# Two row pairs on one vector engine: the first weight sum is ordered behind a low part, and two normalizations are traced later

## The chip, the cores and the metric

The kernel runs on one core of a Trainium2 chip. The core has a matrix engine (TensorE, PE in the profile; its weight loads are listed apart as PEld), a vector engine (VectorE, DVE), a scalar engine (ScalarE, ACT), GpSimd (POOL) and SyncE (SP), which issues the weight transfers. Each engine works through its own list of instructions in order, and the engines wait for each other by semaphores. The metric is the device time of one execution in microseconds; the time before is 2480.34 us, the median of 3 runs (2480.28 to 2482.13).

## What is computed

A decoder trunk of two layers on 256 tokens of width 2048, in float32. Layer 0 is a retention layer with 8 heads and an MLP; layer 1 is a latent attention layer with 16 heads and an MLP. Cut to what matters here:

```python
# layer 0
x = x + retention(rms_norm(x, norm_mix[0]), w_in, w_out)
x = x + square(relu(rms_norm(x, norm_mlp[0]) @ w1)) @ w2
# layer 1
kv     = rms_norm(down) @ w_kv_up                  # per head: 128 of key, 128 of value
k_nope = rms_norm(kv[..., :128]);  v = kv[..., 128:]
q      = rms_norm(h @ w_dq) @ w_uq                 # per head: 128 + 64
q_nope = rms_norm(q[..., :128]); q_pe = rope(rms_norm(q[..., 128:]))
p      = softmax((q_nope @ k_nope + q_pe @ k_pe) * scale, causal)
x = x + (p @ v) @ w_o
x = x + square(relu(rms_norm(x, norm_mlp[1]) @ w1)) @ w2
```

All large products are with weights that are read once from memory: 256 rows against matrices of 2048 to 8192 rows.

## The kernel before

**Splitting.** A float32 weight block is turned into a high part (a cast on ScalarE, L188, into `wh`) and a low part (raw minus high on VectorE, L189, into `wl`). A product of two split numbers is three matmuls: high by high, high by low, low by high (L364 to L366 in the paired products, L248 to L250 in the plain ones). Five buffers each hold `wh` and `wl`, three hold the raw weights (`raw`, 1 MB each), two the sums `us`.

**Row pairs.** `gemm_pair` computes a block of 2 by 2 output tiles. It walks over 8 row pairs; each row pair is one transfer of four 128x512 weight blocks, and is done by `quad`. An 8-product row pair splits the four blocks as they are, in two halves of 1024 columns (part 0 and part 1), and makes 8 products. A 7-product row pair first makes sums of the blocks on VectorE: the first sum (L323, 1024 columns, two sums at once) and two more (L327, L328, 512 columns each). Then it splits four parts: part 0 and part 1 from the raw blocks, part 2 and part 3 from the sums, and makes 7 products. The first low part of a row pair is that of part 0. In a 7-product row pair it is already ordered on VectorE behind the last sum, by `queued_behind`. Which row pairs are of 7 products is written down in lists such as `SEVEN = (3, 5, 7)` and `ODD = (1, 3, 5, 7)`.

**Names.** `u` and `d` are the two products of the MLPs, `rp` and `ro` those of retention, `dqp` and `wop` those of the latent attention; `ku` (keys and values) and `uq` (queries) are plain products, made by `gemm` piece by piece, each piece in two halves.

**What sets the order.** The program is traced in one go; a planner then gives each engine its list. The order of tracing is a rank in this planning: the planner takes the instruction of the lowest rank whose inputs are ready in its own reckoning of time, so an instruction can be put in front of others that were traced earlier. An edge made by `queued_behind` fixes the order of two instructions of one engine and adds no semaphore. The order of tracing itself is set by a small clock: `later(n, fn)` puts a piece of work into a queue with a due time n ticks ahead, and `tick` runs what is due. A row pair is one tick, a half of a plain piece half a tick. A block of queries (`uq`) is 3 pieces, so 3 ticks.

**Keys.** `keyed` takes a finished `ku` block, makes the sums of squares (L964, L965), the root (on GpSimd, L178), multiplies (L970), and has `turn` due 2 ticks later, which transposes the keys on TensorE (kntp).

**Queries.** `query` takes a finished `uq` block b (two heads, 8 blocks): copies and squares on ScalarE (qs, qu), sums of squares on VectorE (L997, L998), the argument of the root (L177, qn_m), the root on GpSimd (L178, qn_r), then the multiplication (L1005), the rotary part (`pe_rope`, L863 to L866) and its split into qpp (L1014, L1015). `turn` is due 3.5 ticks later (2.5 in the last block): it transposes qs and qpp on TensorE (L207: qntp, qptp), and copies to qt and qpe. `score` is due up to 2.5 ticks after that: the scores (s), the mask (L1051), the row maximum (L1056, mx) on VectorE, exponential (L1061) and scaling (L1067) on ScalarE; then p is transposed (ptp, L1074), copied (pt, L1076), and multiplied by the values (ao, L1085; copied to ou, L1089). By these due times `query` of block b and `score` of block b-2 come at the same tick, `query` first. The small tiles of this stage (qs, qu, qpp, p, qt, qpe, pt, ou) share 14 buffers of one tag, `f2k`.

Of the kernel before, what the change touches and what calls it, by code (L numbers as in the profile page):

```python
# [16 lines left out]
ALU = mybir.AluOpType  # L17
# [18 lines left out]
P = 128  # L36
NT = 2
# [6 lines left out]
NOPE, ROPE, MV, KVR, QR = 128, 64, 128, 512, 1536  # L44
# [22 lines left out]
def yoco(ctx: ExitStack, tc: tile.TileContext, a):  # L67
    nc = tc.nc
# [3 lines left out]
    def f2k(shape, name, dtype=F32):  # L72
        return pool.tile([P, *shape], dtype, tag="f2k", bufs=14, name=name)

    def small(w, name):
        return pool.tile([P, w], F32, tag="small", bufs=36, name=name)
# [12 lines left out]
    def act_tile(name, dtype=F32R):  # L89

        return pool.tile([P, 2, 2, S], dtype, tag="act", bufs=24, name=name)


    queue, low_part = [], [None]
    clock, count = [0], itertools.count()

    def later(n, fn):
        queue.append((clock[0] + n, next(count), fn))
# [60 lines left out]
    def gain(col):  # L159
        return gains[:, col : col + 1]  # L160
# [10 lines left out]
    def rstds(total, sizes, name):  # L171

        w = total.free_size()
        m, r = small(w, f"{name}_m"), small(w, f"{name}_r")
        view = m.rearrange("p (t i h) -> p t i h", t=NT, i=len(sizes))
        for i, n in enumerate(sizes):
            nc.vector.tensor_scalar(view[:, :, i], total[:, :, i], 1.0 / n, EPS, op0=ALU.mult, op1=ALU.add)  # L177
        nc.gpsimd.tensor_tensor(r, m, neg_half[:, :w], op=ALU.pow)  # L178
        return r.rearrange("p (t i h) -> p t i h", t=NT, i=len(sizes))
# [104 lines left out]
    def queued_behind(ins, before):  # L284
        tc.add_manual_dep(
            ins.ins, before.ins.name,
            mybir.DependencyInfo(mybir.DependencyClass.NoSync, mybir.DependencyReason.DATA), reason="order",
        )

    def quad(w, chunk, x, mm, name):  # L290

        raw = pool.tile([P, 2048], F32, tag="raw", bufs=3, name=f"{name}_raw")
        nc.sync.dma_start(raw, w[chunk])
        v, more = x

        def a(t, k):
            return [v[:, k, i, t * P : (t + 1) * P] for i in range(2)]

        def s(n):
            return [more[:, n // 2, i, n % 2 * P : (n % 2 + 1) * P] for i in range(2)]  # L300

        def parts(src, n, part, after=None):
            wh = pool.tile([P, 1024], F32R, tag="wh", bufs=5, name=f"{name}_wh{part}")
            wl = pool.tile([P, 1024], F32R, tag="wl", bufs=5, name=f"{name}_wl{part}")
            low = low_part[0] = split(wh[:, : n * 512], wl[:, : n * 512], src)
            if after is not None:
                queued_behind(low, after)
            return [[i[:, j * 512 : (j + 1) * 512] for i in (wh, wl)] for j in range(n)]

        if more is None:  # L310
            b11, b22 = parts(raw[:, 0:1024], 2, 0)
            mm("c11", a(0, 0), b11)
            mm("c21", a(1, 0), b11)
            mm("c12", a(0, 1), b22)
            mm("c22", a(1, 1), b22)
            b12, b21 = parts(raw[:, 1024:], 2, 1)
            mm("c12", a(0, 0), b12)
            mm("c22", a(1, 0), b12)
            mm("c11", a(0, 1), b21)
            mm("c21", a(1, 1), b21)  # L320
            return
        u = [pool.tile([P, 2, 512], F32, tag="us", bufs=2, name=f"{name}_u{i}") for i in range(2)]
        nc.vector.tensor_tensor(  # L323
            u[0], raw[:, 0:1024].rearrange("p (i n) -> p i n", i=2),
            raw[:, 1024:1536].unsqueeze(1).to_broadcast([P, 2, 512]), op=ALU.add,
        )
        nc.vector.tensor_tensor(u[1][:, 0], u[0][:, 0], raw[:, 512:1024], op=ALU.add)  # L327
        summed_up = nc.vector.tensor_tensor(u[1][:, 1], u[1][:, 0], raw[:, 1536:], op=ALU.add)  # L328
        b11, b22 = parts(raw[:, 0:1024], 2, 0, summed_up)
        mm("p1", a(0, 0), b11)  # L330
        mm("c12", s(3), b22)
        (b21,) = parts(raw[:, 1536:], 1, 1, summed_up)
        mm("c11", a(0, 1), b21)
        u2, u4 = parts(u[1].rearrange("p i n -> p (i n)"), 2, 2)
        mm("c21", a(1, 1), u4)
        mm("p6", s(2), u2)
        u1, u3 = parts(u[0].rearrange("p i n -> p (i n)"), 2, 3)
        mm("p5", s(1), u1)
        mm("p7", s(0), u3)
# [378 lines left out]
    act, r = [], []  # L718
# [233 lines left out]
    def keyed(acc, b):  # L952
        if b % 2 == 0:
            vs.append(act_tile(f"v{b}", F32))
        vt = vs[-1][:, b % 2].rearrange("p t (h c) -> p t h c", h=2)
        v_s.append(vt)
        kr = []
        s2 = small(2 * NT, f"skn{b}").rearrange("p (t i h) -> p t i h", t=NT, i=1)
        for t in range(NT):
            src = acc[t].rearrange("p (h c) -> p h c", h=2)  # L960
            k = f2k([2, 2, NOPE], f"kn{b}{t}")
            nc.scalar.activation(k[:, 0], src[:, :, 0:NOPE], AF.Copy, scale=rc[t])
            nc.scalar.activation(vt[:, t], src[:, :, NOPE:], AF.Copy, scale=rc[t])
            nc.vector.tensor_tensor(k[:, 1], k[:, 0], k[:, 0], op=ALU.mult)  # L964
            nc.vector.reduce_sum(s2[:, t, 0], k[:, 1], axis=AX.X)  # L965
            kr.append(k)
        rn = rstds(s2, [NOPE], f"kn{b}")
        for t in range(NT):
            k = kr[t]
            nc.vector.tensor_tensor(  # L970
                k[:, 1], k[:, 0], rn[:, t, 0].unsqueeze(2).to_broadcast([P, 2, NOPE]), op=ALU.mult
            )

        def turn():
            tp = transposed(lambda t, j: kr[t][:, 1, j], f"kntp{b}")
            kt = act_tile(f"kt{b}")
            split(kt[:, 0], kt[:, 1], tp, gain(G_KN))
            k_t.append(kt)

        later(2, turn)  # L980
# [6 lines left out]
    o_act = []  # L987

    def query(acc, b):
        qr, qu = [], []  # L990
        sq = small(4 * NT, f"sq{b}").rearrange("p (t i h) -> p t i h", t=NT, i=2)
        for t in range(NT):
            q = f2k([2, 192], f"qs{b}{t}")
            nc.scalar.activation(q.rearrange("p h c -> p (h c)"), acc[t], AF.Copy, scale=rq[t])
            u = f2k([2, 192], f"qu{b}{t}")
            nc.scalar.activation(u.rearrange("p h c -> p (h c)"), acc[t], AF.Square, scale=rq[t])
            nc.vector.reduce_sum(sq[:, t, 0], u[:, :, 0:NOPE], axis=AX.X)  # L997
            nc.vector.reduce_sum(sq[:, t, 1], u[:, :, NOPE:], axis=AX.X)  # L998
            qu.append((q, u))
        r = rstds(sq, [NOPE, ROPE], f"qn{b}")  # L1000
        for t in range(NT):
            q, u = qu[t]
            for i, cols in enumerate((slice(0, NOPE), slice(NOPE, NOPE + ROPE))):
                n = cols.stop - cols.start
                nc.vector.tensor_tensor(  # L1005
                    q[:, :, cols], q[:, :, cols], r[:, t, i].unsqueeze(2).to_broadcast([P, 2, n]), op=ALU.mult
                )
            flat = u.rearrange("p h c -> p (h c)")
            pe = flat[:, 0 : 2 * ROPE]
            tmp = flat[:, 2 * ROPE : 4 * ROPE].rearrange("p (h c) -> p h c", h=2)  # L1010
            pe_rope(pe.rearrange("p (h c) -> p h c", h=2), tmp, q[:, :, NOPE:], t, 1, 2)
            parts = f2k([2, 2, ROPE], f"qpp{b}{t}", F32R)
            pe = pe.rearrange("p (h c) -> p h c", h=2)
            nc.vector.tensor_copy(parts[:, :, 0], pe)  # L1014
            nc.vector.tensor_tensor(parts[:, :, 1], pe, parts[:, :, 0].bitcast(F32), op=ALU.subtract)  # L1015
            qr.append((q, parts.bitcast(F32)))

        def turn():
            tp = transposed(lambda t, j: qr[t][0][:, j, 0:NOPE], f"qntp{b}")
            raw = f2k([2, S], f"qt{b}")  # L1020
            nc.scalar.activation(raw, tp, AF.Copy, scale=gqn)
            qt = [f2k([2, S], f"qt{b}{i}", F32R) for i in range(2)]
            split(qt[0], qt[1], raw)
            tp = transposed(lambda t, j: qr[t][1][:, j].rearrange("p i c -> p (i c)"), f"qptp{b}")
            qpe = f2k([2, S], f"qpe{b}", F32R)
            nc.scalar.copy(qpe, tp)
            later(2.5 if b < 6 else (1.5 if b < 7 else 1), lambda: score(b, qt, qpe))

        later(2.5 if b == 7 else 3.5, turn)

    def score(b, qt, qpe):

# [64 lines left out]
    act, r = [], []  # L1097
# [107 lines left out]
```

## Time and profile before

| | |
|---|---|
| median of 3 runs | 2480.34 us |
| profiled execution | 2490.9 us, its span 2489.1 us |
| mean granted TensorE clock | 0.996 |
| TensorE busy | 2458.4 us (99%) |
| VectorE busy | 2199.3 us (88%) |
| ScalarE busy | 1647.9 us (66%) |
| GpSimd busy | 232.0 us (9%) |

The profile is one execution, traced by the hardware. A row of the timeline is: start in us from the beginning of the span, duration in us, engine, line of the kernel, operation, tile written and tiles read, shape, and in brackets the idle time in front of it with what ended it. A row of the view of waits is: engine, tile and line that waited, what it waited for, us in all, times, longest. A row of the view of stretches is: from and to, length, then the busy time of PE, PEld, DVE, ACT and POOL with the number of instructions, the granted TensorE clock as a share of full speed, the share of the DMA engines and GB/s. Matmuls overlap in the records: one of 512 columns is listed with 0.39 us.

### The profile page before, as it was taken

To read this page: it belongs to the slowest core of one execution; us is meant where nothing else is said; L and a number is where in the kernel's file an instruction comes from. 1 tells how busy PE (TensorE), PEld (TensorE's weight loads), DVE (VectorE), ACT (ScalarE), POOL (GpSimd) and SP (SyncE) were. 2 spreads that over 40 slices of the span, in tenths; PEclk is the share of its full clock that TensorE was granted. 3 is DMA by queue.
4 is the path that set the end of the run, shared out by engine and by line. 5 is a ranking of instruction groups with operands and counts; after the bars stand their busy time and mean duration, and the time that the engine had idled before them with its cause. 6 is when DMAs were issued, how large, how long until landed. Compare 5 with 4: busy or idle time off the path is not lost.

```text
span 2489.1 us, 31657 instructions
## 1 busy us (share of the span) xinstructions
PE 2458.4 (99%) x11614; PEld 2064.2 (83%) x11614; DVE 2199.3 (88%) x2894; ACT 1647.9 (66%) x2301; POOL 232.0 (9%) x287
## 2 busy tenths in 40 slices
PE   9999999999999999999999999999999999999999
PEld 7888887888888888888888888997888788888887
DVE  7899989989899989989999998776999899899896
ACT  6566656556676767666667777666677567676663
POOL 6200001000000010010110001100000100100100
PEclk9999999999999999999999999999999999999999
DMA  8555568555565685785785565444555866866864
GB/s 311 201 196 190 200 190 252 190 194 207 197 236 187 201 251 207 226 238 197 245 261 204 190 207 177 156 148 156 192 204 200 237 214 199 252 201 225 256 212 167
DMA packets 93403, 521.04 MB, mean 209 GB/s; under 512 B 11072, under 2 KB 12224, under 8 KB 40000
## 3 DMA queue, kind: packets, MB, share of 16 engines
q1 hardware_dynamic: 71856, 472.83, 54.2%
q0 software_dynamic: 21248, 46.15, 8.8%
q8 instruction: 91, 1.49, 0.2%
q14 instruction: 64, 0.52, 0.1%
q10 hardware_dynamic: 144, 0.05, 0.0%
HBM read 479.14 MB, written 39.85 MB: 209 GB/s over the span
## 4 chain that ended last, share of the span: by engine, by line
PE 81%; DVE 7%; DMA 5%; issue 3%; POOL 2%; ACT 2%; DVEq 0%; SPq 0%; ACTq 0%; POOLq 0%
PE u_c L365 7%; PE u_c L366 6%; PE u_c L364 6%; PE d_c L365 5%; PE d_c L366 5%; PE d_c L364 5%; PE rp_c L365 3%; PE rp_c L366 3%; PE rp_c L364 3%; PE rk_acc L276 2%; PE rq_acc L276 2%; PE u_p L366 2%; PE u_p L365 2%; DMA d_raw<-in_mlp_w 2%; PE u_p L364 2%
## 5 line engine op out<-in xcount | busy, mean ns | idle before, releaser
L189 DVE TENSOR_TENSOR d_wl<-d_raw,d_wh 128x1024 fp32r<-128x1024 f32 (+1 forms) x256 | 279.1, 1115 | 27.8 <-ACT d_wh L188 27.8
L188 ACT CAST d_wh<-d_raw 128x1024 fp32r<-128x1024 f32 (+1 forms) x256 | 241.8, 975 | 83.6 <-PE d_c L366 49.5
L189 DVE TENSOR_TENSOR u_wl<-u_raw,u_wh 128x1024 fp32r<-128x1024 f32 (+1 forms) x256 | 277.3, 1111 | 16.8 <-ACT u_wh L188 16.8
L188 ACT CAST u_wh<-u_raw 128x1024 fp32r<-128x1024 f32 (+1 forms) x256 | 240.6, 972 | 70.3 <-PE u_c L366 51.0
L365 PE MATMUL u_c<-u_wl,n 128*128 128x512 f32 x712 | 278.6, 391 | 4.0 <-DVE u_wl L189 4.0
L364 PE MATMUL u_c<-u_wh,n 128*128 128x512 f32 x712 | 278.9, 392 | 0.0
L366 PE MATMUL u_c<-u_wh,n 128*128 128x512 f32 x712 | 278.0, 391 | 0.0
L365 PE MATMUL d_c<-d_wl,hid 128*128 128x512 f32 x660 | 257.8, 391 | 4.1 <-DVE d_wl L189 4.0
L364 PE MATMUL d_c<-d_wh,hid 128*128 128x512 f32 x660 | 259.1, 393 | 0.0
L366 PE MATMUL d_c<-d_wh,hid 128*128 128x512 f32 x660 | 257.7, 390 | 0.0
L188 ACT CAST u_wh<-u_u 128x1024 fp32r<-128x1024 f32 x104 | 107.7, 1054 | 112.0 <-DVE u_u L328 53.3
L188 ACT CAST d_wh<-d_u 128x1024 fp32r<-128x1024 f32 x100 | 104.0, 1055 | 100.4 <-DVE d_u L328 55.8
L365 PEld LDWEIGHTS u_c<-u_wl,n 128*128 128x128 f32 x712 | 134.1, 188 | 33.9 <-DVE u_wl L189 6.7
L366 PEld LDWEIGHTS u_c<-u_wh,n 128*128 128x128 f32 x712 | 134.0, 188 | 27.6
L364 PEld LDWEIGHTS u_c<-u_wh,n 128*128 128x128 f32 x712 | 134.2, 188 | 27.4
L365 PEld LDWEIGHTS d_c<-d_wl,hid 128*128 128x128 f32 x660 | 124.4, 189 | 31.2 <-DVE d_wl L189 6.0
L188 ACT CAST rp_wh<-rp_raw 128x1024 fp32r<-128x1024 f32 x112 | 103.9, 945 | 66.3 <-PE rp_c L366 43.1
L366 PEld LDWEIGHTS d_c<-d_wh,hid 128*128 128x128 f32 x660 | 124.2, 188 | 25.7
L364 PEld LDWEIGHTS d_c<-d_wh,hid 128*128 128x128 f32 x660 | 124.4, 188 | 25.4
L189 DVE TENSOR_TENSOR u_wl<-u_u,u_wh 128x1024 fp32r<-128x1024 f32 x104 | 124.0, 1220 | 9.5 <-ACT u_wh L188 9.4
L189 DVE TENSOR_TENSOR rp_wl<-rp_raw,rp_wh 128x1024 fp32r<-128x1024 f32 x112 | 118.4, 1085 | 4.1 <-ACT rp_wh L188 3.9
L189 DVE TENSOR_TENSOR d_wl<-d_u,d_wh 128x1024 fp32r<-128x1024 f32 x100 | 118.9, 1219 | 2.5 <-ACT d_wh L188 2.4
(566 smaller groups left out, 6579.0 us busy)
## 6 DMA issues: line engine op xcount, KB each, us to landing
u_raw<-in_mlp_w SPq DMA_DIRECT2D x128, 1024.0 KB, 5.5
d_raw<-in_mlp_w SPq DMA_DIRECT2D x120, 1024.0 KB, 4.9
rp_raw<-in_ret_w_gv SPq DMA_DIRECT2D x56, 1024.0 KB, 4.9
ro_raw<-in_ret_w_out SPq DMA_DIRECT2D x32, 1024.0 KB, 5.0
uq_raw<-in_mla_w_uq SPq DMA_DIRECT2D x24, 768.0 KB, 4.2
rq_raw<-in_ret_w_qk SPq DMA_DIRECT2D x16, 1024.0 KB, 5.4
rk_raw<-in_ret_w_qk SPq DMA_DIRECT2D x16, 1024.0 KB, 4.9
xh<-d_c POOLq DMA_DIRECT2D x48, 256.0 KB, 6.2
```

The lines of the kernel that those rows point to most:

```text
L188: nc.scalar.copy(h, src)
L189: return nc.vector.tensor_tensor(l, src, h.bitcast(F32), op=ALU.subtract)
L276: nc.tensor.matmul(acc[f], wh[:, cols], a.rearrange("p i s -> p (i s)"), start=k == 0, stop=k == nk - 1)
L364: nc.tensor.matmul(dst, ah, bh, start=n == 0, stop=False)
L365: nc.tensor.matmul(dst, ah, bl, start=False, stop=False)
L366: nc.tensor.matmul(dst, al, bh, start=False, stop=n == total[key] - 1)
```

## The change

Three edits.

1. `quad` remembers the first low part of the last row pair (`first_low`), and the first sum of a 7-product row pair is ordered behind it on VectorE.
2. In `keyed` the multiplication by the root is traced 0.5 tick later, as `normed`.
3. In `query` what follows the root (multiplication, rotary part, split) becomes `rotated`, traced 1.5 ticks later (1 in the last block); `turn` is then due 2 ticks after that (1.5 in the last block), so 3.5 and 2.5 ticks after `query` as before.

```diff
-    queue, low_part = [], [None]
+    queue, low_part, first_low = [], [None], [None]
...
             low = low_part[0] = split(wh[:, : n * 512], wl[:, : n * 512], src)
             if after is not None:
                 queued_behind(low, after)
+            if part == 0:
+                first_low[0] = low
...
-        nc.vector.tensor_tensor(
+        first_sum = nc.vector.tensor_tensor(
             u[0], raw[:, 0:1024].rearrange("p (i n) -> p i n", i=2),
             raw[:, 1024:1536].unsqueeze(1).to_broadcast([P, 2, 512]), op=ALU.add,
         )
+        if first_low[0] is not None:
+            queued_behind(first_sum, first_low[0])
...
         rn = rstds(s2, [NOPE], f"kn{b}")
-        for t in range(NT):
-            k = kr[t]
-            nc.vector.tensor_tensor(
-                k[:, 1], k[:, 0], rn[:, t, 0].unsqueeze(2).to_broadcast([P, 2, NOPE]), op=ALU.mult
-            )
+
+        def normed():
+            for t in range(NT):
+                k = kr[t]
+                nc.vector.tensor_tensor(
+                    k[:, 1], k[:, 0], rn[:, t, 0].unsqueeze(2).to_broadcast([P, 2, NOPE]), op=ALU.mult
+                )
+
+        later(0.5, normed)
...
         r = rstds(sq, [NOPE, ROPE], f"qn{b}")
+        later(1 if b == 7 else 1.5, lambda: rotated(b, qu, r))
+
+    def rotated(b, qu, r):
+        qr = []
         for t in range(NT):
...
-        later(2.5 if b == 7 else 3.5, turn)
+        later(1.5 if b == 7 else 2, turn)
```

More of the change, by code (lines that the diff above doesn't have):

```diff
@@ L989, in query @@
     def query(acc, b):
-        qr, qu = [], []
+        qu = []
         sq = small(4 * NT, f"sq{b}").rearrange("p (t i h) -> p t i h", t=NT, i=2)
```

## The prediction

> **What bounds the kernel now.** I read the page first: the span, and which engine fills it.
>
> ```profile
> span 2489.1 us, 31657 instructions
> PE 2458.4 (99%) x11614; PEld 2064.2 (83%) x11614; DVE 2199.3 (88%) x2894; ACT 1647.9 (66%) x2301; POOL 232.0 (9%) x287
> ```
>
> TensorE (PE) is busy for all but 30.7 us of 2489.1. No matmul is added or removed, so the change can win only what TensorE loses: its idle time, and time at a lower clock. VectorE (DVE), at 88%, is the next engine; work put on it later can still become a wait of TensorE. So the second view is the waits of TensorE alone (columns: total us, times, longest).
>
> ```profile
> PE d_c L365 <- DVE d_wl L189: 4.0, 3, 2.0
> PE u_c L365 <- DVE u_wl L189: 4.0, 5, 1.8
> PE ptp L1074 <- ACT p L1067: 3.6, 2, 3.4
> PE ptp L1074 <- ACT ou L1089: 2.2, 3, 0.9
> PE rp_c L365 <- DVE rp_wl L189: 1.8, 1, 1.8
> PE ro_c L365 <- DVE ro_wl L189: 1.1, 2, 0.7
> PE ao L1085 <- ACT pt L1076: 1.0, 1, 1.0
> PE ptp L1074 <- ACT qpe L1026: 0.3, 2, 0.2
> ```
>
> There are two families. In the paired products (d, u, rp, ro) TensorE waits for a low part (L189): 4.0 + 4.0 + 1.8 + 1.1 = 10.9 us. In the attention part it waits for softmax and copies on ScalarE (ACT): 3.6 + 2.2 + 1.0 + 0.3 = 7.1 us. The waits of the other engines say what stands behind each.
>
> ```profile
> DVE d_u L323 <- DMA d_raw<-in_mlp_w: 21.9, 12, 4.0
> DVE u_u L323 <- DMA u_raw<-in_mlp_w: 20.2, 16, 3.8
> ACT p L1061 <- DVE mx L1056: 31.3, 8, 6.3
> DVE qs L1005 <- POOL qn_r L178: 13.5, 8, 1.8
> DVE kn L970 <- POOL kn_r L178: 4.9, 8, 1.1
> ```
>
> VectorE stands at the first weight sum (L323) for weights that have not landed, and ScalarE stands up to 6.3 us for a row maximum (L1056). The timeline shows one place of each kind. First the costliest low-part wait: VectorE, then ScalarE's casts, then TensorE.
>
> ```profile
> 1938.11 2.35 DVE L189 TENSOR_TENSOR d_wl<-d_u,d_wh 128x1024 fp32r<-128x1024 f32 x2
> 1944.44 1.23 DVE L323 TENSOR_TENSOR d_u<-d_raw 128x1024 f32<-128x1024 f32 x1 [3.98 <-DMA d_raw<-in_mlp_w]
> 1945.70 0.69 DVE L327 TENSOR_TENSOR d_u<-d_u,d_raw 128x512 f32<-128x512 f32 x1
> 1946.31 2.35 DVE L189 TENSOR_TENSOR d_wl<-d_raw,d_wh 128x1024 fp32r<-128x1024 f32 x2
> 1948.58 0.69 DVE L328 TENSOR_TENSOR d_u<-d_u,d_raw 128x512 f32<-128x512 f32 x1
> ...
> 1940.70 1.05 ACT L188 CAST d_wh<-d_raw 128x1024 fp32r<-128x1024 f32 x1 [1.65 <-PE d_c L366]
> 1942.02 1.05 ACT L188 CAST d_wh<-d_raw 128x1024 fp32r<-128x1024 f32 x1 [0.26 <-PE d_c L366]
> ...
> 1945.22 0.39 PE L364 MATMUL d_c<-d_wh,hid 128*128 128x512 f32 x1
> 1947.59 0.50 PE L365 MATMUL d_c<-d_wl,hid 128*128 128x512 f32 x1 [1.98 <-DVE d_wl L189]
> ```
>
> The sum at 1944.44 belongs to a 7-product row pair. The two low parts at 1946.31 belong to the 8-product row pair in front of it; their casts were done at 1941.75 and 1943.07. They stood behind a sum that TensorE does not need yet.
>
> Now one period of the query stage: VectorE, then ScalarE's wait, then the end of the scores on TensorE.
>
> ```profile
> 1669.27 0.29 DVE L177 TENSOR_SCALAR qn_m<-sq 128x4 f32<-128x4 f32 x2
> 1671.30 0.96 DVE L1005 TENSOR_TENSOR qs<-qs,qn_r 128x256 f32<-128x256 f32 x3 [1.75 <-POOL qn_r L178]
> ...
> 1674.20 0.95 DVE L189 TENSOR_TENSOR uq_wl<-uq_raw,uq_wh 128x768 fp32r<-128x768 f32 x1
> 1675.07 0.22 DVE L1014 CAST qpp<-qu 128x128 fp32r<-128x128 f32 x1
> 1675.20 0.42 DVE L1051 TENSOR_TENSOR p<-s,cst 128x256 f32<-128x256 f32 x1
> 1675.54 0.28 DVE L1015 TENSOR_TENSOR qpp<-qu,qpp 128x128 fp32r<-128x128 f32 x1
> 1675.74 0.68 DVE L1051 TENSOR_TENSOR p<-s,cst 128x512 f32<-128x512 f32 x1
> ...
> 1676.84 0.40 ACT L1061 ACTIVATE p<-p,mx 128x128 f32<-128x128 f32 x1 [4.44 <-DVE mx L1056]
> ...
> 1665.86 0.40 PE L1046 MATMUL s<-kpe_t,qpe 128*128 128x256 f32 x2
> ```
>
> The scores s of an older block are finished at 1666.26, yet the mask (L1051) starts at 1675.20: in front of it VectorE waits 1.75 us for GpSimd's root (L178) and rotates a newer block's query. Last, the granted clock (in the stretches below, the number before the two DMA columns).
>
> ```profile
> 1700.50:1710.00 9.50, 8.22 (x34) 7.38 (x35) 4.28 (x4) 5.88 (x11) 0.00 (x0) 0.52 0.37 123
> 1948.60:1952.00 3.40, 3.40 (x9) 2.64 (x8) 3.40 (x5) 1.10 (x2) 0.85 (x1) 0.51 0.66 176
> 1952.00:1957.00 5.00, 5.00 (x23) 4.13 (x22) 4.05 (x5) 2.95 (x3) 0.86 (x1) 1.00 1.03 347
> 1992.00:1996.40 4.40, 4.31 (x12) 3.44 (x13) 4.40 (x6) 1.04 (x1) 0.86 (x1) 0.61 0.47 117
> ```
>
> Behind the longest waits TensorE runs at about half its clock for 3 to 10 us. That loss counts as busy on the page.
>
> **The change part by part.** *First sum behind a low part.* Nothing is computed more or less; an edge fixes the order of two VectorE instructions, without a semaphore. Where the sum already follows, nothing changes. Where it leads, sum and first low part swap: the low part comes 1.23 us plus the sum's wait earlier, the sum at most 1.22 us later, everything behind both at the same time. In the place above the first low part would run at 1941.8, and TensorE would find it at 1945.45. The second low part is still behind the sum: 1944.44 + 1.23, perhaps L327 (0.69), then 2.35 / 2 = 1.18 for one low part: ready near 1947.5. TensorE needs it 12 matmuls after 1945.45. By the stretch with 23 matmuls in 5.00 us that is 12 x 0.22 = 2.6 us, so 1948.1. It fits with 0.6 us to spare, and with no margin if the weights were another 0.6 us later. What is queued behind the waiting sum is now the second low part, L327 and L328, and behind these the casts of the sums. Order and number of the weight transfers on SP's queue stay; the raw buffer is let go about 1.2 us earlier. Worth in this execution: 10.9 us of idle, and the half clock behind the two longest waits, 3.40 x 0.49 = 1.7 and 4.40 x 0.39 = 1.7, together 3.4: 14.3 us.
>
> *Rotation of the query put off by 1.5 ticks (1 in the last block).* No instruction is added; turn and score stay due when they were. The mask of the older block is traced ahead of the rotation instead of behind it. The first mask row stands directly behind the second L1014, the write that takes the last new buffer of the rotation, so I read that buffers of this tag are handed out in the order of tracing, and that the mask was held by this. Without it the mask can follow L177 at 1669.56. From mask to exponential it is 1676.84 - 1675.20 = 1.64 us, so the exponential would start near 1671.2, 5.6 us earlier. That is more than the longest ptp wait (3.4). The copies qpe and ou stand behind the exponentials on ScalarE and come earlier with them. What stays is the wait of ao (1.0): pt is copied behind ptp in either order; I also keep 0.5 of the rest. Half clock from 1700.50 to 1710.00: 8.22 x 0.48 = 3.9 us. Worth: 7.1 - 1.5 + 3.9 = 9.5 us.
>
> *Key normalization put off by 0.5 tick.* It takes VectorE out of a 4.9 us wait in all, and no TensorE wait names it: 0. Its cover is the slack in front of the key transposes, where TensorE shows no wait.
>
> *One rule of the clock.* The Trainium skill (TensorE: Matmul & The Clock Gate, section "What's actually happening") says that half rate follows at least one idle window of about 3.4 us. The trace does not agree: a wait of 1.98 us was followed by 0.51. By that page neither half-clock term would exist, and the sum below would be 2490.9 - 10.9 - 5.6 = 2474.4 us.
>
> *The sum.* The profiled execution took 2490.9 us: 2490.9 - 14.3 - 9.5 = 2467.1. The median of the runs shown is 2480.34, 10.6 us less. These runs show no trace, so the first term is bounded there from both sides: if all 10.6 us are weights that landed later under the profiler, 14.3 - 10.6 = 3.7 us are left; if none are, 14.3. Landing is what differs between like places (12 and 16 of the d and u sums waited, by up to 4.0 us), while the query stage is a chain of computing that repeats. So I take a value near the lower end, 5.3 us: 2480.3 - 9.5 - 5.3 = 2465.5 us.
>
> **The rivals.** *Slower: the rotation comes too late for its transposes.* Its last write ends at 1675.82, and the transposes that read it start here:
>
> ```profile
> 1688.43 0.60 PE L207 MATMUL qptp<-cst,qpp 128*128 128x128 f32 x4
> ...
> 1594.55 2.33 POOL qn_r L178
> 1612.85 1.65 POOL qn_r L178
> ```
>
> The slack is 12.6 us. A period, by the two roots, is 18.3 us for 3 ticks, so 1.5 ticks are 9.2 us; 3.4 us are left, and 1.75 us more as the root is no longer waited for. It decides once VectorE gives the rotation another 5.2 us of queue. If each of 8 blocks were 3 us late: 2465.5 + 24 = 2489.5 us. For it: VectorE also has the weights' low parts to do there. Against: by the page 12% of VectorE's time is free, and the 1.75 us wait is freed for them.
>
> *The rotation does not move.* The edges of the first part are fixed, but `later` only changes a rank. If the mask still follows the rotation because the planner thinks the scores late, the 9.5 us stay: 2475.0 us. For it: a weight's low part (1674.20), ranked behind the mask, was put in front of it. Against: the mask follows the same L1014 too exactly.
>
> *The transfers were on time without the profiler.* Then the first part is worth 0: 2470.8 us.
>
> *All the stalls of the trace are there without the profiler:* 2480.3 - 9.5 - 14.3 = 2456.5 us.
>
> *The root gets slower.* It took 2.33 us where a low part ran on VectorE in the same moment, and 1.65 us where VectorE stood still. Now low parts will run under all 8: 8 x 0.68 = 5.4 us; if the chain behind it set the pace, 2470.9 us. I expect it hidden by the tick or more that the rotation now waits. The Trainium skill (GPSIMD Engine Reference, section "Specifications") states the like: GpSimd shares its SBUF interfaces with VectorE, and instructions with two SBUF inputs contend. The trace agrees by these two rows.
>
> **How the numbers follow.** Chances: the forecast (2460 to 2470) 0.48; all stalls (2454 to 2460) 0.13; transfers on time or the slower root (2470 to 2473) 0.16; the rotation does not move (2473 to 2479) 0.11; nothing gained (2479 to 2485) 0.05; slower 0.07. What a measurement can tell here is 0.2%, 5.0 us: below 2475.4 is faster. Of the fifth case half lies below it, so faster 0.48 + 0.13 + 0.16 + 0.06 = 0.83, within 0.2% 0.10, slower 0.07. The range leaves out the last two cases and the ends of their neighbours: 2456 to 2477.
>
> **What would show it.** In the profile after: L323's waits for DMA may stay, but TensorE's waits for d_wl, u_wl, rp_wl and ro_wl should fall from 10.9 us to under 2, and the clock of the MLP stay at 1.00. L1051 should stand ahead of L1005 in each period, ScalarE's 31.3 us wait for mx fall below 15, L1005's 13.5 us wait for qn_r go, and the 3.4 us wait of ptp with the half clock after it vanish. The forecast is wrong if qntp or qptp begin to wait, if a sum's wait holds the second low part, or if the order of the query stage is the old one.

## The result, and the profile after

The changed kernel takes 2464.08 us (median of 6 runs, 2462.67 to 2466.32), the kernel before 2480.27 us on the same chip (2475.36 to 2482.13). The ratio is 0.9932, with a 95% interval of 0.9918 to 0.9946: 16 us less. A second measurement of the same kernel, with the last experiments, gave 2464.11 us and 0.9921 (0.9905 to 0.9937). The forecast was 2465.5 us.

The profiled execution of the changed kernel took 2466.32 us, that of the kernel before 2490.9. Two rows of the first part of the page:

```profile
span 2464.5 us, 31657 instructions
PE 2446.7 (99%) x11614; PEld 2062.5 (84%) x11614; DVE 2192.3 (89%) x2894; ACT 1648.4 (67%) x2301; POOL 238.0 (10%) x287
```

The span fell by 24.6 us (2489.1 to 2464.5). The same 11614 matmuls fill 11.7 us less (2458.4 to 2446.7): that is time which TensorE had spent busy at a lower clock or in stretched matmuls. The other 12.9 us are idle time (30.7 to 17.8). Both kinds went, as the prediction had them, though not in its proportions (below).

The waits of TensorE after (columns: total us, times, longest):

```profile
PE rg_acc L248 <- ACT a L190: 5.4, 1, 5.4
PE sc L675 <- DVE rk_q L659: 3.7, 2, 2.9
PE kd_acc L249 <- DVE kd_wl L189: 2.1, 2, 1.2
PE uq_acc L249 <- DVE uq_wl L189: 0.9, 1, 0.9
PE ao L1097 <- ACT pt L1088: 0.5, 1, 0.5
```

The four rows of low parts in the paired products (d, u, rp, ro; 10.9 us before) are gone, and so are the rows of ptp (3.6 + 2.2 + 0.3). Of the attention's 7.1 us, 0.5 are left. The row of rg_acc stood there before too, with 5.6 us. New are sc, 86 us into the run, kd_acc and uq_acc; they are taken up among the experiments. The other engines' waits, again of after:

```profile
DVE d_u L325 <- DMA d_raw<-in_mlp_w: 3.8, 4, 1.6
DVE u_u L325 <- DMA u_raw<-in_mlp_w: 3.7, 6, 0.9
ACT p L1073 <- DVE mx L1068: 15.4, 7, 2.6
DVE qs L1017 <- POOL qn_r L178: 5.2, 5, 1.5
DVE kn L976 <- POOL kn_r L178: 4.9, 8, 1.1
```

The first sums of the MLPs (L323 before, L325 now) waited 21.9 + 20.2 us for weights before and wait 7.5 now. Much of this idle time of VectorE has only moved: its low parts (L189) of d, u, rp and ro, which now stand in front of the sums, wait 117.4 us for their casts, and waited 81.4 before. The sum that waited 3.98 us in the prediction's place, the 111th of 150, is this one in the timeline of after:

```profile
1928.91 1.23 DVE L189 TENSOR_TENSOR d_wl<-d_raw,d_wh 128x1024 fp32r<-128x1024 f32 x1 [0.43 <-ACT d_wh L188]
1930.36 1.23 DVE L325 TENSOR_TENSOR d_u<-d_raw 128x1024 f32<-128x1024 f32 x1 [0.22 <-DMA d_raw<-in_mlp_w]
1931.50 1.22 DVE L189 TENSOR_TENSOR d_wl<-d_raw,d_wh 128x1024 fp32r<-128x1024 f32 x1
```

The first low part is through before VectorE meets the sum, the weights are 0.22 us late instead of 3.98, and the second low part follows. One period of the query stage after, VectorE first, then GpSimd's root and ScalarE's exponential:

```profile
1645.89 0.29 DVE L177 TENSOR_SCALAR qn_m<-sq 128x4 f32<-128x4 f32 x2
1646.09 1.02 DVE L1063 TENSOR_TENSOR p<-s,cst 128x256 f32<-128x256 f32 x2
1647.02 1.00 DVE L1068 TENSOR_REDUCE mx<-p 128x2 f32<-128x256 f32 x2
1647.99 0.96 DVE L1017 TENSOR_TENSOR qs<-qs,qn_r 128x256 f32<-128x256 f32 x3
...
1646.32 1.64 POOL L178 TENSOR_TENSOR qn_r<-qn_m,neg_half 128x8 f32<-128x8 f32 x1 [14.96 <-DVE qn_m L177]
...
1647.46 0.41 ACT L1073 ACTIVATE p<-p,mx 128x128 f32<-128x128 f32 x1 [2.13 <-DVE mx L1068]
```

Mask (L1063) and row maximum (L1068) now stand between L177 and the rotation (L1017). They take 1.9 us, the time that the root needs (1646.32 + 1.64 = 1647.96), so L1017 starts without a wait. From L177 to the exponential it is 1647.46 - 1645.89 = 1.57 us; before it was 1676.84 - 1669.27 = 7.57.

By stretches (columns as in the prediction: from and to, length, busy time of PE, PEld, DVE, ACT, POOL, granted clock, DMA share, GB/s), first the query stage and the second MLP of before, then the same of after:

```profile
1590.00:1715.00 125.00, 117.76 (x711) 111.56 (x710) 86.49 (x220) 84.56 (x186) 14.81 (x14) 0.96 0.45 154
1790.00:2460.00 670.00, 663.05 (x2977) 548.44 (x2976) 613.83 (x725) 453.55 (x579) 49.49 (x61) 0.99 0.69 221
```

```profile
1590.00:1715.00 125.00, 123.62 (x768) 117.73 (x768) 92.29 (x231) 93.16 (x206) 14.81 (x14) 1.00 0.47 166
1790.00:2460.00 670.00, 670.00 (x3025) 556.13 (x3023) 610.27 (x719) 447.39 (x565) 50.70 (x59) 1.00 0.69 220
```

The stretches are equally long, not equal in work (711 and 768 matmuls in the first). In 125 us of the query stage TensorE's idle time went from 7.24 to 1.38 us and the clock from 0.96 to 1.00; in 670 us of the MLP from 6.95 us to nothing, and the clock from 0.99 to 1.00.

### The profile page after: what moved, and what is told of

Its sections match the earlier page's. It is cut to its first block, busy times and chain, and to the rows that moved or that the text cites. A ratio compares the mean times of both kernels' runs of the same rounds, so it can differ in the third digit from the quotient of the medians.

```text
span 2464.5 us, 31657 instructions
## 1 busy us (share of the span) xinstructions
PE 2446.7 (99%) x11614; PEld 2062.5 (84%) x11614; DVE 2192.3 (89%) x2894; ACT 1648.4 (67%) x2301; POOL 238.0 (10%) x287
## 4 chain that ended last, share of the span: by engine, by line
PE 94%; POOL 2%; DVE 2%; ACT 1%; DMA 1%; issue 1%; SPq 0%; ACTq 0%
PE u_c L368 7%; PE u_c L370 7%; PE u_c L369 7%; PE d_c L368 6%; PE d_c L370 6%; PE d_c L369 6%; PE rp_c L370 3%; PE rp_c L368 3%; PE rp_c L369 3%; PE u_p L368 2%; PE u_p L369 2%; PE u_p L370 2%; PE rq_acc L276 2%; PE rk_acc L276 2%; PE ro_c L370 2%; PE ro_c L368 2%
## 5 line engine op out<-in xcount | busy, mean ns | idle before, releaser
L189 DVE TENSOR_TENSOR d_wl<-d_raw,d_wh 128x1024 fp32r<-128x1024 f32 (+1 forms) x256 | 280.0, 1114 | 45.6 <-ACT d_wh L188 45.6
L189 DVE TENSOR_TENSOR u_wl<-u_raw,u_wh 128x1024 fp32r<-128x1024 f32 (+1 forms) x256 | 278.8, 1110 | 31.5 <-ACT u_wh L188 31.5
L189 DVE TENSOR_TENSOR rp_wl<-rp_raw,rp_wh 128x1024 fp32r<-128x1024 f32 x112 | 119.1, 1084 | 18.2 <-ACT rp_wh L188 18.0
L189 DVE TENSOR_TENSOR u_wl<-u_u,u_wh 128x1024 fp32r<-128x1024 f32 x104 | 123.1, 1217 | 2.3 <-ACT u_wh L188 1.9
L189 DVE TENSOR_TENSOR d_wl<-d_u,d_wh 128x1024 fp32r<-128x1024 f32 x100 | 118.3, 1216 | 0.5 <-ACT d_wh L188 0.5
```

The costliest lines, as they stand in the source:

```text
L189: return nc.vector.tensor_tensor(l, src, h.bitcast(F32), op=ALU.subtract)
```

## The experiments

My theory had two separate gains: the low parts no longer stand behind a late sum (some 5 us without the profiler), and the masks no longer stand behind the rotation, because its buffers were handed out first (some 10 us). Rivals: the gain is all of one part; the order of tracing isn't what holds the mask; lateness of weights isn't what the sum part removes; and on the slower side, a rotation that comes too late for its transposes.

**Each part alone.** The sum part:

```diff
+            if part == 0:
+                first_low[0] = low
...
+        if first_low[0] is not None:
+            queued_behind(first_sum, first_low[0])
```

> The kernel before with the first edit alone (the edge from the first low part to the first sum). Theory: the whole gain of 16.2 us is the sum of two independent parts, 9.5 us from the query stage and the rest, 6.7 us, from the sums; so this run is at 2473.6 us, between 2471 and 2476. In its profile TensorE's waits for the low parts of d, u, rp and ro (10.9 us before) are under 2 us, VectorE's waits for weights at the first sum (52 us before) under 15, and the attention waits (ptp, ao; 7.1 us) stay. Rival: the weights are late only in a disturbed execution, and the edge is worth nothing in the median: 2480 us, with the whole gain in the query stage.

Measured: 2474.80 us (2473.95 to 2476.16), ratio 0.9978 (0.9968 to 0.9987). Against 2480.17 us of the kernel before that is 5.4 us. Its waits of TensorE in the attention part stay as they were, while those for d_wl and u_wl have no row left (a new one, kd_acc with 2.1 us, is taken up below):

```profile
PE ptp L1078 <- ACT p L1071: 3.6, 2, 3.4
PE ptp L1078 <- ACT ou L1093: 2.2, 3, 0.9
PE ao L1089 <- ACT pt L1080: 1.0, 1, 1.0
PE rp_p L369 <- DVE rp_wl L189: 0.4, 1, 0.4
```

The query part:

```diff
         r = rstds(sq, [NOPE, ROPE], f"qn{b}")
+        later(1 if b == 7 else 1.5, lambda: rotated(b, qu, r))
+
+    def rotated(b, qu, r):
...
-        later(2.5 if b == 7 else 3.5, turn)
+        later(1.5 if b == 7 else 2, turn)
```

> The kernel before with the third edit alone (the rotation traced 1.5 ticks later). Theory: 2480.3 - 9.5 = 2470.8 us, between 2468 and 2473; the mask stands ahead of the rotation, the waits of ptp are gone, and TensorE keeps its full clock at the change from the queries to the output product. The waits for low parts stay as before. Rival (the edge is worth nothing): 2464 us, all of the gain. Rival (the rotation does not move the mask): 2480 us.

Measured: 2469.66 us (2468.59 to 2475.88), ratio 0.9959 (0.9943 to 0.9975): 10.5 us. Here it is the other way round. No ptp row is left, and the low parts still cost TensorE time. They cost 5.2 us, though, and not the 10.9 us that I expected to stay:

```profile
PE d_c L365 <- DVE d_wl L189: 2.9, 2, 1.5
PE u_c L365 <- DVE u_wl L189: 2.1, 2, 1.7
PE ao L1089 <- ACT pt L1080: 0.5, 1, 0.5
PE rp_c L365 <- DVE rp_wl L189: 0.2, 1, 0.2
```

The key part:

```diff
-        for t in range(NT):
...
+        def normed():
+            for t in range(NT):
...
+        later(0.5, normed)
```

> The kernel before with the second edit alone (the key normalization traced 0.5 tick later). Theory: worth nothing, 2480 us within 2; VectorE's 4.9 us of waiting for the root of the keys may go or stay, since TensorE waits for none of it. Rival: it frees VectorE ahead of the query stage and is worth 2 us or more.

Measured: 2480.39 us (2477.88 to 2484.63), ratio 1.0002 (0.9992 to 1.0012). The wait that this edit looks aimed at, 4.9 us before, did not move:

```profile
DVE kn L972 <- POOL kn_r L178: 4.9, 8, 1.1
```

The three parts add up: 5.4 + 10.5 - 0.2 = 15.7 us, against 16.2 us for the whole. Within the spread of these runs neither part needs the other.

**Is it the lateness of weights that the sum part takes away?** The kernel before, with half of the weight bytes of these row pairs:

```diff
-        nc.sync.dma_start(raw, w[chunk])
+        nc.sync.dma_start(raw[:, 0:1024], w[chunk][:, 0:1024])
...
-            raw[:, 1024:1536].unsqueeze(1).to_broadcast([P, 2, 512]), op=ALU.add,
+            raw[:, 0:512].unsqueeze(1).to_broadcast([P, 2, 512]), op=ALU.add,
```

and likewise for the other reads of the second half.

> The kernel before, with the order of its instructions left alone, but each row pair fetches only the first 1024 of its 2048 columns and uses them twice; it leaves out half of the weights of the paired products, and its time is that of the same instructions with weights that land early. Theory (the loss is the wait for late weights at a sum that leads): the first sums wait for nothing, TensorE's waits for low parts go, and the time is that of the edge alone, about 2473 us. Rival (the edge helps by the order itself, since VectorE's own work is what is late): the waits for low parts stay and the time is 2480 us.

Measured: 2473.53 us (2472.36 to 2476.58), ratio 0.9975 (0.9965 to 0.9984), 6.6 us less: about what the sum part gives. What I expected of the sums was wrong, though. They still wait, 38.5 us in all their rows (51.6 before), for up to 2.6 us (ro_u; 2.0 in the costliest row) rather than 4.0. TensorE feels only a little of it:

```profile
DVE u_u L323 <- DMA u_raw<-in_mlp_w: 18.1, 12, 2.0
...
PE rp_c L365 <- DVE rp_wl L189: 1.3, 2, 0.7
PE ro_c L365 <- DVE ro_wl L189: 0.4, 1, 0.4
```

Then the same halving in the kernel after:

> The kernel after, with each row pair of a 7-product set fetching only its first 1024 columns and using them twice; half of the weights is left out. If the sums behind a low part have taken away all that late weights cost, fewer bytes bring nothing more: the time of the kernel after within 2 us, 2462 to 2466 us. If late weights still cost something beside the low parts (VectorE still waits 7.5 us for them), it is 2 to 5 us faster, 2459 to 2462 us.

Beside it ran the kernel after itself:

> The kernel after once more, on the chip of the next two runs, so that they stand beside it: 2464 us within 3 us, with all its executions within 6 us of each other.

Measured: 2464.67 us (2463.26 to 2467.67) with half of the weights, 2464.11 us (2462.92 to 2466.40) with all. Fewer bytes bring nothing any more: what lateness still costs once the sums stand behind a low part is too small to see in executions that spread over some 4 us. The first sums of the halved kernel show a single wait:

```profile
DVE dqp_u L325 <- DMA dqp_raw<-in_mla_w_dqp: 0.9, 1, 0.9
```

**How much room is there behind the sum?** The kernel after, with the sum behind the second low part:

```diff
-            if part == 0:
+            if part == 1:
                 first_low[0] = low
```

> The kernel after, with the first weight sum behind the second low part of the row pair in front, not the first. The prediction found 0.6 us to spare for the second low part behind the sum; here it is the sum that comes later, by a low part of 0.6 to 1.1 us. If the sums have that room, the time is that of the kernel after, 2464 us within 2 us, and TensorE waits for no sum. If they have not, waits of TensorE for the summed weights appear, under 1 us each in some of 150 row pairs, and the time is 2466 to 2480 us.

Measured: 2464.70 us (2462.41 to 2465.37), ratio 0.9943 (0.9928 to 0.9958), and among TensorE's waits one for the weights of a paired product, 0.8 us for wop_wh, where the kernel after has 0.4. A sum that is one more low part late costs nothing that the time shows.

**What held the mask?** The buffers first: the kernel before, with the rotation traced where it always was, but the qpp tiles out of the shared tag.

```diff
-            parts = f2k([2, 2, ROPE], f"qpp{b}{t}", F32R)
+            parts = pool.tile([P, 2, 2, ROPE], F32R, tag="qpp", bufs=2, name=f"qpp{b}{t}")
```

To make room for them, rope_tab and kpe_t share one buffer.

> The kernel before, with the two qpp tiles of a block in buffers of a tag of their own; the rotation is traced where it always was. If the mask stands behind the rotation because its buffer and those of qpp come from one tag and are handed out in the order of tracing, the masks can now be taken up before the root: the ptp waits of TensorE (3.4 us behind the longest of them) go, and most of what the query part gives alone (10.5 us) comes: 2470 to 2473 us. If the rotation's place in tracing itself, or the wait for the root on GpSimd, holds the mask, nothing changes: 2480 us, and the ptp waits stay.

Measured: 2475.49 us (2470.03 to 2489.20), ratio 0.9984 (0.9965 to 1.0002). That lies between my two cases, and the interval reaches from 8.7 us less to no change. The time decides nothing; the timeline does:

```profile
1646.34 0.42 DVE L1051 TENSOR_TENSOR p<-s,cst 128x256 f32<-128x256 f32 x1
1648.25 0.96 DVE L1005 TENSOR_TENSOR qs<-qs,qn_r 128x256 f32<-128x256 f32 x3 [1.49 <-POOL qn_r L178]
...
1650.48 0.69 DVE L1051 TENSOR_TENSOR p<-s,cst 128x512 f32<-128x512 f32 x1
...
1652.28 0.68 DVE L1056 TENSOR_REDUCE mx<-p 128x2 f32<-128x512 f32 x1
```

The first mask row now stands ahead of the root's wait; the second is still among the rotation. TensorE's waits in ptp fell from 6.1 to 1.7 us. So the shared buffers did hold the first mask row, and something else holds the second one. Next the order of tracing alone, with no time put off: the rotation is kept for the same tick and so traced behind the scores of that tick.

```diff
+        later(0, lambda: rotated(b, qu, r))
+
+    def rotated(b, qu, r):
+        qr = []
```

> The kernel before, with the rotation of the queries kept for the same tick, so that it is traced behind the score and attention steps of that tick instead of ahead of them, and the turn where it was. If the order of tracing alone is what holds the mask, this does as much as the move by 1.5 ticks, which alone took 2469.66 us: 2468 to 2472 us, no ptp wait over 0.5 us. If the room of 1.5 ticks is needed, the ptp waits stay and the time is near 2480 us.

Measured: 2473.55 us (2465.90 to 2482.41), ratio 0.9975 (0.9957 to 0.9993). The interval, 1.7 to 10.7 us less, holds what the query part gave alone, but doesn't fix it; the median lies above the 2468 to 2472 us that I expected. In the trace the order is that of the changed kernel, and the rest of the stage follows (no wait of TensorE for ptp is left):

```profile
1646.50 1.01 DVE L1055 TENSOR_TENSOR p<-s,cst 128x256 f32<-128x256 f32 x2
1647.44 1.00 DVE L1060 TENSOR_REDUCE mx<-p 128x2 f32<-128x256 f32 x2
1648.41 0.96 DVE L1009 TENSOR_TENSOR qs<-qs,qn_r 128x256 f32<-128x256 f32 x3
```

Being traced first is what counts, then, and 1.5 ticks are not needed for it. That an earlier-traced instruction also goes first among those that are ready would explain the second mask of the run above; I argued this from the two timelines, and no run shows it by itself.

**The slower side, forced.** The kernel after, with the rotation three ticks late:

```diff
-        later(1 if b == 7 else 1.5, lambda: rotated(b, qu, r))
+        later(2 if b == 7 else 3, lambda: rotated(b, qu, r))
...
-        later(1.5 if b == 7 else 2, turn)
+        later(0.5, turn)
```

> The kernel after, with the rotation 3 ticks late (2 in the last block) and its transposes half a tick behind it, so that they are issued where they were. The rival of the prediction that ends slower, forced: if the transposes then come before the rotated rows, waits of TensorE for qr and qpp appear, 0.5 to 4 us in each of 8 blocks, and the time rises from 2464 us to 2468 to 2490 us. If the rotation still finishes in time, 2464 us and no such wait.

Measured: 2465.39 us (2464.22 to 2467.80), ratio 0.9949 (0.9934 to 0.9963). My expectation was wrong: the wait came, but in one block of eight, 1.4 us in all, and the time stayed under the 2468 us that I had put as the least. The timeline of VectorE, then of TensorE:

```profile
1646.03 0.28 DVE L1027 TENSOR_TENSOR qpp<-qu,qpp 128x128 fp32r<-128x128 f32 x1
...
1647.74 0.95 DVE L1017 TENSOR_TENSOR qs<-qs,qn_r 128x256 f32<-128x256 f32 x3
...
1610.07 0.30 PE L207 MATMUL qptp<-cst,qpp 128*128 128x128 f32 x1 [0.46 <-DVE qpp L1027]
1611.31 0.55 PE L207 MATMUL qptp<-cst,qpp 128*128 128x128 f32 x3 [0.94 <-DVE qpp L1027]
...
1646.61 0.60 PE L207 MATMUL qptp<-cst,qpp 128*128 128x128 f32 x4
```

The multiplication L1017 stands where it stood in the kernel after (1647.74 against 1647.99), although it was traced 1.5 ticks later. Only the writes into qpp moved, into the next period, and there they end 0.3 us before their transposes (1646.31, 1646.61). In the kernel after they end 11.6 us before (the later of the two L1027 here ends at 1653.19):

```profile
1652.71 0.48 DVE L1027 TENSOR_TENSOR qpp<-qu,qpp 128x128 fp32r<-128x128 f32 x2
...
1664.80 0.60 PE L207 MATMUL qptp<-cst,qpp 128*128 128x128 f32 x4
```

So the rival exists, but it begins about where this run stands, not at 1.5 ticks.

**Is there more to have?** In the changed kernel the writes into qpp stand behind the split of qt, which waits for ScalarE. The kernel after, with qpp in a tag of its own (the edit shown above):

> The kernel after, with the qpp tiles in a tag of their own, so that the casts into qpp need not stand behind the split of qt, which waits 1.1 us for ScalarE in each block. TensorE waits for nothing there any more, so the time should stay: 2464 us within 2 us. If those 1.1 us still reach TensorE in some block, 1 to 4 us faster.

Measured: 2463.86 us (2463.12 to 2465.06), against 2464.11 us for the kernel after on the same chip: the same. VectorE's wait was hidden.

**The new wait at the start.** The sc wait at 86 us (2.9 us, and 3.40 us at half clock behind it) stands in a stretch where VectorE's and ScalarE's instructions have the same order in both kernels, behind an x0s copy that was 1.6 us later than in the profiled execution of before (it waited 2.65 us for its transfer from in_xt). It differs from run to run: 3.7, 3.2, 1.9, 3.0, 2.6, 2.8 and 1.1 us in the seven profiles with the sum part, and 0, 0.6, 2.1, 0.7, 0.2 and 2.0 us in the six without it. The two groups overlap, yet lie apart in the mean (2.6 and 0.9). Whether the sum part has a share in it stays open.

**Two more new waits.** The kd_acc wait comes with the sum part: 2.1 us in all seven profiles that have it, no row in the six that don't. In the kernel after, the first low part of kd stands behind five additions to x_mlp, although its cast was done at 1401.86:

```profile
1403.14 2.49 DVE L489 TENSOR_TENSOR x_mlp<-d_c,x_mlp 128x512 f32<-128x512 f32 x4
...
1406.76 0.81 DVE L189 TENSOR_TENSOR kd_wl<-kd_raw,kd_wh 128x640 fp32r<-128x640 f32 x1
```

In the kernel before it stood behind the first of these additions. So the edge, which takes one low part out from behind work that nobody needs yet, came with a plan that puts another one there; why the planner chose it, no run shows. The uq_acc wait (0.3 to 0.9 us) is there in all eight profiles with a rotation that is traced later and in none of the other five.

## Why the prediction was right, point by point

**The bound.** Right: what was won is what TensorE lost, in the two families named. Predicted for the profiled execution: 16.5 us of idle time (10.9 + 5.6) and 7.3 us of half clock, 23.8 in all. Measured: 12.9 of idle, 11.7 of busy time, 24.6 in all. In the rows named, 17.5 us of idle time went (10.9 in the low parts, 6.6 in the attention), and 2.6 us more in small rows that I had not counted; but 7.3 us came anew (3.7 for sc, 2.1 for kd_acc, 0.9 for uq_acc, 0.6 in two small rows), and the prediction had no term for a wait that the change brings. Of the busy time, 4.1 us went in the plain part of the output product (62.4 to 58.3), where I had counted 3.9 of half clock, and 4.5 us from there to the end (725.4 to 720.9), where I had counted 3.4; 1.8 us in the first MLP and 1.1 us in the queries I had not counted. That busy time fell by the most where the half clock stood decides for the trace on the rule of the clock: without half-clock terms the sum was 2474.4 us, with them 2467.1, and the profiled execution took 2466.3. That the last two lie so close is luck: the idle term was 3.6 us too large and the busy term 4.4 us too small.

**The sum part.** The forecast took 5.3 us from a range of 3.7 to 14.3; alone it gave 5.4. The choice near the lower end held: the profiled execution of before, from which the 14.3 came, lies near the top of that kernel's executions (2474.1 to 2491.9 in all runs here). In the four other profiles without the sum part and with all weights, TensorE's waits for these low parts come to 5.2, 2.8, 4.4 and 4.9 us, where that execution had 10.9. So it was this execution that was late, and not every execution under the profiler, as the prediction had it. That 5.3 met 5.4 is luck: nothing in the prediction fixed the value within its range, and the measured one has an interval of 3.2 to 7.9 us. "It fits with 0.6 us to spare" was not put to the test. In the place that it was worked out for, the weights came only 0.22 us late, and the run with the sum behind the second low part takes that low part out of the sum's way; it shows room for the sum, not for the low part. No profile with the sum part has a wait of TensorE above 0.4 us for a low part of d, u, rp or ro.

**The query part.** 9.5 us predicted, 10.5 measured alone (6.2 to 14.1 by its interval). The reading that buffers are handed out in the order of tracing held for the first mask row, and the order of tracing for both. The exponential came 7.57 - 1.57 = 6.0 us earlier; 5.6 was the estimate. Two expectations of detail failed. ScalarE's wait for mx fell to 15.4 us, not below 15 (and a 4.5 us wait of the first block stands in another row): in each later period ScalarE still stands 2.1 to 2.6 us while VectorE does mask and maximum behind L177. And L1017's wait for qn_r did not go, it fell from 13.5 to 5.2: the first three blocks have no older block's mask ahead of L1017 to fill the root's time, and wait 1.53 us each.

**The step that failed** is that of the slower rival: "a period is 18.3 us for 3 ticks, so 1.5 ticks are 9.2 us; 3.4 us are left". A tick is a place in the tracing, not a time. The rotation starts 2.10 us behind L177 after (1645.89, 1647.99), and 2.03 us before (1669.27, 1671.30); the slack of its transposes went from 12.6 to 11.6 us. I gave that rival 0.07, which was enough, for a wrong reason.

**The slower root** did not come. The root's eight instructions in before, then in after (columns: least, median and most ns):

```profile
L178 POOL TENSOR_TENSOR qn_r<-qn_m,neg_half x8: 1635/1648/2315, 1569.1 to 1690.4; 128x8 f32<-128x8 f32 x8
```

```profile
L178 POOL TENSOR_TENSOR qn_r<-qn_m,neg_half x8: 1636/1648/2316, 1566.3 to 1682.2; 128x8 f32<-128x8 f32 x8
```

What moved beside the root is the mask and the maximum, not a weight's low part, and beside these it takes its 1.64 us. "Low parts will run under all 8" was wrong.

**The key part:** 0 predicted, 0 measured (between 2.0 us less and 3.0 us more by its interval).

## What to carry to other kernels

When an engine takes its work in a fixed order, look at what stands in front of the instruction that the bound engine waits for: here two instructions that nobody needed yet, a sum of weights still in flight and a rotation waiting for a root, cost TensorE 16 us. An order edge or a change in the order of tracing removes that without adding work. Then look for waits that the new order brings; here it was 2.1 us at kd_acc. How far "later" moves something is read from a trace, not from a count of ticks.

## What the runs showed of the hardware

The kernels with the sum part scatter less than those without it. From lowest to highest, with the number of runs: 3.7 us (6), 3.5 (6), 2.2 (11), 3.6 (4), 3.0 (4), 4.4 (6) and 1.9 (6) with it; 7.3 (6), 6.8 (12), 19.2 (10) and 16.5 (10) without, and 6.8 (6), 11.6 (29), 17.8 (19) and 13.4 (11) in the kernel before itself. With half of the weights and without the sum part it is 4.2 (11). This points to late weights that reach TensorE as most of the scatter: the edge bought steadiness as well as 5 us.

The half clock does not follow from the length of the wait in front of it. The same eight matmuls sc stand behind a wait in the changed kernel, in that with the own tag added, and in that with the sum behind the second low part:

```profile
86.44 2.84 PE L675 MATMUL sc<-rq_q,rk_q 128*128 128x256 f32 x8 [2.87 <-DVE rk_q L659]
```

```profile
85.47 2.70 PE L675 MATMUL sc<-rq_q,rk_q 128*128 128x256 f32 x8 [1.91 <-DVE rk_q L659]
```

```profile
86.73 1.57 PE L675 MATMUL sc<-rq_q,rk_q 128*128 128x256 f32 x8 [2.63 <-DVE rk_q L659]
```

They took 2.84 and 2.70 us behind 2.87 and 1.91 us, but 1.57 us behind 2.63. Closer still: 2.84 us behind 2.04 with the rotation kept for the same tick, 1.57 us behind 2.07 with the key part alone. In the first case the clock reads 0.50 over the 3.40 us from 86.60:

```profile
86.60:90.00 3.40, 3.40 (x12) 2.94 (x13) 3.40 (x4) 0.12 (x1) 0.00 (x0) 0.50 0.31 60
```

The Trainium skill (TensorE: Matmul & The Clock Gate, section "What's actually happening") says that the window of about 3.4 us in which activity is watched runs freely and is not reset when a kernel starts. A stretch of 3.40 us and the same wait ending either way agree with that; no run here shows the window itself. The same section asks for a whole idle window ahead of the half rate; the 1.91 us here speak against that.
